# A hybrid backbone: where two groups of modulation weights and the latents are loaded in the opening stage

## The chip, the cores and the metric

The kernel runs on one core of one Trainium2 chip. The metric is the time of one execution on the device in microseconds, lower is better. The median of three runs of the kernel before is 4596.12 us (4592.82 to 4600.3). The profile is that of one further execution.

Five engines have instruction lists of their own and run them in order: TensorE (PE in the rows; PEld is its loading of weights), VectorE (DVE), ScalarE (ACT), GpSimd (POOL) and SyncE (SP). Transfers between memory and the core's own memory are issued either by SP (queue q1 in the rows) or by POOL (queue q0); the same 16 DMA engines move the bytes of both. An issue that has to wait, for a buffer for instance, holds back what stands behind it on its engine.

## The reference, cut to what matters

A two-layer backbone over 512 latent tokens x, with 256 context tokens in front, model width 1024, all in float32. Layer 0 mixes with a short convolution beside a state-space scan, layer 1 with a gated linear recurrence; an expert stage follows in each layer.

```
cond_x = silu(c); cond_c = silu(c_ctx)
mx = split(cond_x @ ada_w[layer] + ada_b[layer], 6)     # ada_w[layer]: 1024 x 6144
mc = split(cond_c @ ada_w[layer] + ada_b[layer], 6)
hx = modulate(rmsnorm(x,   norm_mix_w[layer]), mx[0], mx[1])
hc = modulate(rmsnorm(ctx, norm_mix_w[layer]), mc[0], mc[1])
ox, oc = even_mixer(hx, hc, ...)                         # layer 0
x   = x   + mx[2] * ox;   ctx = ctx + mc[2] * oc
x   = x   + mx[5] * peer_ffn(modulate(rmsnorm(x, ...), mx[3], mx[4]), ...)
ctx = ctx + mc[5] * peer_ffn(modulate(rmsnorm(ctx, ...), mc[3], mc[4]), ...)
```

Six vectors of 1024 are computed from each layer's modulation weights. The context's mixer needs the first two before anything else, the third when it adds its result, the last three only in the expert stage. The latents' mixer starts from the context's final states, so the context's mixer comes first.

## The kernel before, in words

**The opening.** The context (two tiles of 128 tokens, `cx`) is loaded, normed and transposed (`context_raw`, L274). The modulation weights of a layer are 24 MB and are handled in three groups of 2048 columns (`ada_group`, L242). Group 0 gives the first two vectors, group 1 the third and fourth, group 2 the fifth and sixth. A group has 16 tiles `adaw` of 128 x 1024 floats (0.52 MB each), with six buffers that all groups share, and two matmuls for each tile (L263), 32 in all; each has only the 32 columns of `cond` as its weights and writes one quarter of the rows of a PSUM tile. Then VectorE adds the bias (L265), and four small stores put the vectors into memory (`mods`). `context_mod` (L284) applies group 0 to the transposed context and splits it into a high and a low part (`hTch`, `hTcl`).

**The context's mixer** (`even_mixer`, L435, with 256 tokens). Every projection is three matmuls for a k (high by high, low by high, high by low; L229) with weights `ev_w_in` that are loaded into `wr` (four buffers) and split into `wh` and `wl` by ScalarE and VectorE (L199, L200). `even_steps` comes first (`step_sizes`, L361). Then, for each half: two groups of the state-space scan (`ssd`, L495: projections, transposes L515, L522, the decay terms L553 to L574, a group norm L589), the short convolution of four blocks (`short_conv`, L476: projections only), and the output projection (`out_proj`, L456, matmuls L469 with `ev_w_out`), whose gate needs group 1.

**What sets the order.** The program is traced in the order of the code, and a scheduler then puts each engine's instructions into an order of its own, by what depends on what and by its own idea of time. Two helpers bind it. `tc.issue_after(ins)` puts each instruction of its block behind `ins`, but only those on the same engine as `ins`. `between(todo, hooks)` (L305) spreads a list of pieces of work over calls of `hook` (L297); each `hook` follows an instruction of VectorE (in `ssd` L570, one for each of two tiles; in `short_conv` L493) and runs the pieces that are due in an `issue_after` of that instruction. `HA` (L29) is the number of hooks over which the pieces are spread.

In the kernel before, groups 1 and 2 are such pieces, with their tiles on SP's queue behind the last tile of group 0 (`rows` is that DMA); the latents' four tiles `x` are loaded by SP behind it as well. The latents are first read when their own mixer begins, after the context's.

Of the kernel before, what the change touches and what calls it, by code (L numbers as in the profile page):

```python
# [25 lines left out]
HF = 2  # L26
FD, TU = 0, 0
HB = 4
HA = 6  # L29
GA = (1, 3, 7)  # L30
NA0 = 12
NA1, NS1, W1, NR1, HS1, HS0, NE1 = 30, 8, 34, 6, 100, 96, 4
# [33 lines left out]
class Backbone:  # L66
# [1349 lines left out]
    def build(self):  # L1416
        tc, nc, io = self.tc, self.nc, self.io
        with ExitStack() as es:
# [7 lines left out]
            x = [hold.tile([128, D], F32, name=f"x{i}") for i in range(4)]  # L1426
            self.ctxd = [tc.dram_tile((T_C, D), F32, name=f"ctx{l}") for l in range(2)]

            @contextmanager
            def phase(bufs, raws=2):  # L1430

                with tc.tile_pool(name="wpool", bufs=bufs) as self.wpool:
                    self.rawp = self.wpool, raws
                    yield
# [51 lines left out]
            with phase(4, 4):  # L1486
                ada_pool = right("ada")
                C = ada_pool.__enter__()
                for i in range(2):
                    self.load(cx[i], io["ctx"][i * 128:(i + 1) * 128])  # L1490
                with tc.tile_pool(name="evenhc", bufs=1) as H:
                    with tc.tile_pool(name="prec0", bufs=1) as Q:
                        hT = self.split_pair(H, [128, KT, T_C], "hTc")
                        xT = self.context_raw(cx, Q)
                        ada = self.ada_group(0, 0, C, 6)
                        with tc.issue_after(ada.ins):
                            self.even_consts(H, T_C)
                            self.context_mod(xT, hT, Q)
                    rows = ada

                    def ada_group(l, j):
                        with tc.issue_after(rows.ins):
                            self.ada_group(l, j, C, 6)

                    self.between([lambda l=l, j=j: ada_group(l, j)
                                  for l, j in ((0, 1), (0, 2))], HA)
                    with Pools(tc, "evenc") as P:
                        with tc.issue_after(ada.ins):
                            steps = self.even_steps(hT, T_C, P, "c")
                        with tc.issue_after(rows.ins):  # L1510
                            for i in range(4):
                                self.load(x[i], io["x"][i * 128:(i + 1) * 128])
                        with tc.issue_after(ada.ins):
                            fin = self.even_mixer(hT, T_C, T_C, steps, None, cx, P, "c")
                self.dump("cm0", cx)
                for i in range(2):
                    self.load(self.ctxd[0][i * 128:(i + 1) * 128], cx[i])
                ada_pool.__exit__(None, None, None)
                ch = right("c_h")
                ctoks, hW = self.context_norm(E, ch.__enter__(), cx)  # L1520
# [83 lines left out]
```

## Time and profile before

| | |
|---|---|
| median of three runs | 4596.12 us |
| the profiled execution | 4590.89 us |
| its span, first to last instruction | 4589.1 us |
| TensorE busy | 4199.3 us, 92% of the span |
| VectorE, ScalarE, POOL busy | 3420.0, 1755.9, 1456.6 us |
| mean DMA rate | 244 GB/s |
| modulation tiles of layer 0, by SP | 48 of 0.52 MB |
| modulation tiles of layer 1, by POOL | 48 of 0.52 MB |

The change concerns the opening and the context's mixer, the first 330 us or so. In the rows, a matmul of 32-bit floats appears as two records (`x4` are two matmuls of L263), one of L229 as a single one. The shares of the whole span say little of this stage, so the rows below are of stretches of it.

### The profile page before, as it was taken

Reading aid. Unit: us, or ns where it says so; the run is one execution under the profiler, and the core shown is the slowest. Engines: PE = TensorE matmul, PEld = TensorE weight load, DVE = VectorE, ACT = ScalarE, POOL = GpSimd, SP = SyncE. Lnnn points to the kernel's source line nnn. Section 1 sums busy time; section 2 is a strip of 40 time slices with the busy share of each in tenths; the row PEclk is TensorE's granted clock in tenths of the full one; section 3 lists DMA queues with packets and bytes.
Section 4 is the critical chain, followed back from the end, with each engine's and each line's share of the span. In section 5 each row is a group of like instructions: output and inputs, shape, how many; then the busy total and the mean of one; then the engine's idle time right before and its main releaser. Section 6 shows DMA issues by size and latency. Waiting matters only on the chain. (4 is left out here: it accounts for less than half of the span.)

```text
span 4589.1 us, 60329 instructions
## 1 busy us (share of the span) xinstructions
PE 4199.3 (92%) x21452; PEld 3358.1 (73%) x21452; DVE 3420.0 (75%) x6826; ACT 1755.9 (38%) x3155; POOL 1456.6 (32%) x1114
## 2 busy tenths in 40 slices
PE   7999868868897889999999999998999999999998
PEld 5666635535443778888899988887757779888997
DVE  4556887786676989977888875666896558878887
ACT  4442321321223833333333345554447533333333
POOL 0002244444435355544545410000000005445543
PEclk9999979969998989999999999998999999999999
DMA  9538778878777899988988941111246758989886
GB/s 315 175 111 274 237 230 270 262 227 289 248 250 261 267 326 351 363 330 317 321 325 321 338 138 52 57 60 49 83 139 193 235 193 320 328 305 330 327 315 224
DMA packets 488766, 1119.52 MB, mean 244 GB/s; under 512 B 39792, under 2 KB 252336, under 8 KB 488464
## 3 DMA queue, kind: packets, MB, share of 16 engines
q1 hardware_dynamic: 334096, 553.55, 36.0%
q0 software_dynamic: 154368, 562.11, 34.9%
q8 instruction: 169, 2.77, 0.2%
q14 instruction: 133, 1.09, 0.1%
HBM read 1054.18 MB, written 60.82 MB: 243 GB/s over the span
## 5 line engine op out<-in xcount | busy, mean ns | idle before, releaser
L952 POOL DMA_INDIRECT g<-in_peer_u_dram,idx x256 | 372.4, 1455 | 923.1 <-DVE pre L1057 693.6
L229 PE MATMUL yp<-hTh,wh 128*128 128x384 f32 x1808 | 610.3, 338 | 12.9 <-ACT wh L199 11.7
L200 DVE TENSOR_TENSOR wl<-wr,wh 128x1024 fp32r<-128x1024 f32 x404 | 493.1, 1221 | 167.1 <-ACT wh L199 162.6
L229 PE MATMUL yp<-hTh,wl 128*128 128x384 f32 x1808 | 611.5, 338 | 5.4 <-DVE wl L200 5.2
L229 PE MATMUL yp<-hTl,wh 128*128 128x384 f32 x1808 | 608.1, 336 | 0.0
L199 ACT ACTIVATE wh<-wr 128x1024 fp32r<-128x1024 f32 x404 | 426.1, 1056 | 443.5 <-DMA wr<-in_peer_uT_dram 181.2
L952 POOL DMA_INDIRECT g<-in_peer_v_dram,idx x256 | 392.3, 1533 | 376.4 <-DVE y L1077 309.8
L952 POOL DMA_INDIRECT g<-in_peer_v_dram,idxc x256 | 339.1, 1325 | 392.4 <-DVE y L1077 172.9
L1057 DVE CUSTOM_DVE_ANT_0 g<-g,cx 128x1024 f32<-128x1024 f32 x256 | 312.7, 1223 | 148.3 <-DMA g<-in_peer_u_dram,idxc 145.9
L952 POOL DMA_INDIRECT g<-in_peer_u_dram,idxc x256 | 289.8, 1132 | 390.8 <-DVE prec L1057 343.5
L200 DVE TENSOR_TENSOR vl<-wr,vh 128x1024 fp32r<-128x1024 f32 x256 | 312.4, 1220 | 70.2 <-ACT vh L199 70.0
L229 PEld LDWEIGHTS yp<-hTh,wh 128*128 128x128 f32 x1808 | 341.5, 189 | 25.6 <-ACT wh L199 13.5
L229 PE MATMUL mm<-hTh,wh 128*128 128x512 f32 (+1 forms) x864 | 343.9, 399 | 17.3 <-ACT yT L579 8.6
L229 PEld LDWEIGHTS yp<-hTh,wl 128*128 128x128 f32 x1808 | 340.9, 189 | 13.1 <-DVE wl L200 10.1
L1057 DVE CUSTOM_DVE_ANT_0 g<-g,h 128x1024 f32<-128x1024 f32 x256 | 305.9, 1221 | 59.2 <-DMA g<-in_peer_u_dram,idx 59.0
L229 PEld LDWEIGHTS yp<-hTl,wh 128*128 128x128 f32 x1808 | 341.3, 189 | 8.9
L229 PE MATMUL mm<-hTh,wl 128*128 128x512 f32 (+1 forms) x864 | 342.1, 398 | 2.5 <-DVE wl L200 2.3
L229 PE MATMUL mm<-hTl,wh 128*128 128x512 f32 (+1 forms) x864 | 340.8, 395 | 0.2 <-DVE hTl L200 0.2
L1353 DVE TENSOR_TENSOR a<-a,gt 128x384 f32<-128x384 f32 x256 | 215.3, 845 | 167.3 <-ACT a L1241 91.4
L199 ACT ACTIVATE vh<-wr 128x1024 fp32r<-128x1024 f32 x256 | 270.2, 1055 | 173.4 <-PE mc L1375 76.4
L1077 DVE SCALAR_TENSOR_TENSOR y<-g,pre,y 128x1024 f32<-128x1024 f32 x254 | 325.1, 1280 | 13.0 <-DMA g<-in_peer_v_dram,idx 11.6
L88 POOL TENSOR_TENSOR rs_y<-rs_v,mhalf 128x1 f32<-128x1 f32 (+2 forms) x29 | 24.3, 839 | 929.6 <-DVE rs_v L87 929.5
(462 smaller groups left out, 9665.7 us busy)
## 6 DMA issues: line engine op xcount, KB each, us to landing
wr<-in_peer_v_dram SPq DMA_DIRECT2D x256, 512.0 KB
wr<-in_peer_uT_dram SPq DMA_DIRECT2D x226, 512.0 KB
gd<-stage SPq DMA_DIRECT2D x24, 2048.0 KB
gt<-gd SPq DMA_DIRECT2D x64, 768.0 KB
wr<-in_ev_w_in_dram SPq DMA_DIRECT2D x80, 512.0 KB
adaw<-in_ada_w_dram SPq DMA_DIRECT2D x48, 512.0 KB
adaw<-in_ada_w_dram POOLq DMA_DIRECT2D x48, 512.0 KB
wr<-in_peer_wq_dram SPq DMA_DIRECT2D x40, 512.0 KB
```

The costliest lines, as they stand in the source:

```text
L88: nc.gpsimd.tensor_tensor(y, v, self.mhalf[:, :n], op=OP.pow)
L199: self.nc.scalar.activation(hi, src, AF.Copy)
L200: self.nc.vector.tensor_sub(lo, src, hi.bitcast(F32))
L229: mm(o, a, rhs(kk, i)[b], start=first and kk == 0 and n == 0, stop=last and kk == k - 1 and n == 2)
L952: self.nc.gpsimd.indirect_dma_start(out=g, out_offset=None, in_=table, in_offset=bass.IndirectOffsetOnAxis(ap=idx, axis=0), element_offset ...
L1057: self.nc.vector.tensor_tensor_reduce(g, g, t.h2, 1.0, 0.0, OP.mult, OP.add, s["pre"][:, k, h:h + 1])
L1077: nc.vector.scalar_tensor_tensor(t.y, g, a, t.y, op0=OP.mult, op1=OP.add)
L1353: self.last = nc.vector.tensor_mul(a, a, self.gt_[:, :, i % 4])
```

## The change

```
-HA = 6
+HA = 12
...
-                    rows = ada
-
-                    def ada_group(l, j):
-                        with tc.issue_after(rows.ins):
-                            self.ada_group(l, j, C, 6)
-
-                    self.between([lambda l=l, j=j: ada_group(l, j)
-                                  for l, j in ((0, 1), (0, 2))], HA)
+
+                    def load_x():
+                        for i in range(4):
+                            nc.gpsimd.dma_start(x[i], io["x"][i * 128:(i + 1) * 128])
+
+                    self.between([lambda j=j: self.ada_group(0, j, C, 6, nc.gpsimd) for j in (1, 2)] + [load_x], HA)
                     with Pools(tc, "evenc") as P:
                         with tc.issue_after(ada.ins):
                             steps = self.even_steps(hT, T_C, P, "c")
-                        with tc.issue_after(rows.ins):
-                            for i in range(4):
-                                self.load(x[i], io["x"][i * 128:(i + 1) * 128])
```

The tiles of groups 1 and 2 are issued by POOL instead of SP, and the extra `issue_after` around them is gone. Three pieces (group 1, group 2, the latents) are spread over twelve hooks instead of two over six, so they are traced at hooks 1, 5 and 9. The latents' four loads are issued by POOL and are the third piece.

At the start of POOL's list, rows of the difference (`x_88` to `x_91` are the latents' tiles, `rs_y` belongs to the context's first norm):

```order
 L163 IOTA jp 128x128
 L182 IOTA iota_82 128x128
+L1502 DMA x_88<-in_x_dram 128x1024
+L1502 DMA x_89<-in_x_dram 128x1024
+L1502 DMA x_90<-in_x_dram 128x1024
+L1502 DMA x_91<-in_x_dram 128x1024
 L88 TENSOR_TENSOR rs_y<-rs_v,mhalf 128x2
 L341 IOTA iot 128x4
 L347 IOTA iop 128x1
+L262 DMA adaw<-in_ada_w_dram 128x1024 x32
```

The latents' loads are now the first transfers on POOL, and all tiles of groups 1 and 2 follow in one run.

On TensorE between the two groups of the scan in the first half (from the first group's norm L589 to the second group's L553), the kernel before:

```order
L589 MATMUL mc<-yT,ones 128x256 x2
L515 MATMUL mc<-ident,ch 128x128 x3
L263 MATMUL mm<-adaw,cond 32x512 x4
L522 MATMUL mc<-xe,tk 128x512
L515 MATMUL mc<-ident,ch 128x128 x3
L263 MATMUL mm<-adaw,cond 32x512 x4
L522 MATMUL mc<-xe,tk 128x512
L553 MATMUL mc<-ch 128x128
```

and the changed one:

```order
L589 MATMUL mc<-yT,ones 128x256 x2
L515 MATMUL mc<-ident,ch 128x128 x3
L522 MATMUL mc<-xe,tk 128x512
L515 MATMUL mc<-ident,ch 128x128 x3
L522 MATMUL mc<-xe,tk 128x512
L553 MATMUL mc<-ch 128x128
```

The matmuls of group 2 that stood between the scan's steps are gone from there. On TensorE at the start of the short convolution, and within it, the kernel before has projections only (the first rows; `mm_1344` is a PSUM tile):

```order
L589 MATMUL mc_1224<-yT_432,ones_80 128x256 x2
L229 MATMUL mm_1344<-hTch_127,wh_1304 128x256
L229 MATMUL mm_1344<-hTcl_128,wh_1304 128x256
L229 MATMUL mm_1344<-hTch_127,wl_1305 128x256
L229 MATMUL mm_1344<-hTch_127,wh_1304 128x256
```

and the changed one, a stretch in its middle (`mm_1329` is the PSUM tile of group 2):

```order
L263 MATMUL mm_1329<-adaw_1366,cond_99 32x512 x2
L229 MATMUL mm_1447<-hTch_127,wh_1442 128x256
L229 MATMUL mm_1447<-hTcl_128,wh_1442 128x256
L229 MATMUL mm_1447<-hTch_127,wl_1443 128x256
L229 MATMUL mm_1447<-hTch_127,wh_1442 128x256
L229 MATMUL mm_1447<-hTcl_128,wh_1442 128x256
L263 MATMUL mm_1329<-adaw_1370,cond_99 32x512 x2
```

Group 2 now stands among the projections of the short convolution: a run of twelve matmuls and then ten pairs. Before the first L561 the kernel before has 48 matmuls of groups 1 and 2 in 16 places (runs of 8, 6 and 4 among them) and 336 projection matmuls; the changed one has the 32 of group 1 there, as a run of twelve, eight pairs and a run of four, and 352 projection matmuls. On TensorE the sixteen transposes of the context (L128), which the kernel before mixes into group 0, now stand ahead of all of it.

## Rows read from the trace of the kernel before

**Rows 1.** Busy times by stretch: us, busy PE, PEld, DVE, ACT, POOL, PEclk, DMA share, GB/s

```profile
0.00:34.00 34.00, 19.87 (x80) 5.12 (x80) 5.64 (x27) 10.94 (x14) 1.54 (x9) 0.95 0.87 292
41.40:116.60 75.20, 70.54 (x471) 52.38 (x471) 36.29 (x69) 35.90 (x53) 0.00 (x0) 0.94 0.98 325
116.60:155.20 38.60, 31.89 (x222) 18.02 (x220) 20.87 (x40) 18.27 (x30) 0.00 (x0) 0.96 0.53 183
155.20:185.00 29.80, 29.76 (x248) 29.76 (x249) 20.19 (x33) 15.62 (x20) 0.00 (x0) 1.00 0.56 155
```

**Rows 2.** TensorE in order of time: start, us, then the wait before it

```profile
33.24 1.05 PE L263 MATMUL mm<-adaw,cond 128*32 128x512 f32 x4 [0.28 <-DMA adaw<-in_ada_w_dram]
...
39.41 0.39 PE L229 MATMUL mc<-hTch,wh 128*128 128x256 f32 x1 [2.79 <-ACT hTch L199]
...
116.68 0.38 PE L561 MATMUL mc<-trow,srow 15*128 15x512 bf16 x1
...
155.24 0.38 PE L229 MATMUL mm<-hTch,wh 128*128 128x256 f32 x1 [0.93 <-ACT scx L482]
...
185.09 1.45 PE L469 MATMUL mc<-wo,yT 128*128 128x512 f32 x3
```

**Rows 3.** Busy times of two short stretches

```profile
41.90:46.40 4.50, 4.50 (x23) 4.50 (x23) 3.60 (x8) 2.12 (x2) 0.00 (x0) 0.50 1.14 339
346.00:350.00 4.00, 4.00 (x14) 3.30 (x13) 3.75 (x7) 1.20 (x2) 3.54 (x7) 0.50 0.82 275
```

**Rows 4.** TensorE's waits from 41.5 to 185: us in total, times, longest

```profile
PE mc L589 <- ACT yT L586: 4.0, 2, 2.2
...
PE mm L229 <- ACT wh L199: 0.5, 1, 0.5
```

**Rows 5.** SP's and POOL's lists in order of time

```profile
7.49 0.71 POOL L88 TENSOR_TENSOR rs_y<-rs_v,mhalf 128x2 f32<-128x2 f32 x1 [6.21 <-DVE rs_v L87]
...
33.69 2.00 SPq L81 DMA_DIRECT2D x<-in_x_dram  x4
...
40.05 2.77 SPq L262 DMA_DIRECT2D adaw<-in_ada_w_dram  x3
...
346.29 3.44 POOL L262 DMA_DIRECT2D adaw<-in_ada_w_dram  x6 [0.18 <-issue]
```

**Rows 6.** ScalarE in order of time, the first use of the latents

```profile
339.46 1.04 ACT L111 ACTIVATE hin<-x 128x1024 f32<-128x1024 f32 x1
```

**Rows 7.** Busy times of two stretches of the opening

```profile
3.00:18.00 15.00, 8.14 (x32) 3.34 (x36) 3.62 (x14) 7.80 (x12) 0.92 (x3) 1.00 1.02 347
18.00:25.00 7.00, 3.90 (x24) 0.64 (x20) 0.00 (x0) 1.86 (x2) 0.00 (x0) 1.00 0.86 267
```

**Rows 8.** DMA queues from 350 to 356: packets, MB, share of 16 engines

```profile
q0 software_dynamic: 399, 1.47, 78.9%
q1 hardware_dynamic: 315, 0.41, 23.3%
```

**Rows 9.** TensorE in order of time, four and two modulation matmuls together

```profile
63.53 1.06 PE L263 MATMUL mm<-adaw,cond 128*32 128x512 f32 x8
...
74.05 1.05 PE L263 MATMUL mm<-adaw,cond 128*32 128x512 f32 x4
```

**Rows 10.** Busy times of L263 alone by stretch: PE, PEld, PEclk, DMA share, GB/s

```profile
41.40:116.60 75.20, 18.46 (x96) 2.87 (x96) 0.94 0.98 325
116.60:155.20 38.60, 6.06 (x34) 0.80 (x32) 0.96 0.53 183
```

**Rows 11.** TensorE and VectorE within the scan, in order of time

```profile
131.79 1.83 PE L589 MATMUL mc<-yT,ones 128*128 128x256 f32 x4 [2.16 <-ACT yT L586]
...
140.09 1.10 PE L522 MATMUL mc<-xe,tk 128*128 128x512 f32 x2 [1.83 <-DVE xe L520]
...
146.88 0.69 DVE L568 TENSOR_TENSOR E<-E,ch 128x512 f32<-128x512 f32 x1
...
149.94 0.66 PE L574 MATMUL yp<-E,tk 128*64 128x128 f32 x8
```

## The prediction

> **What bounds the kernel now.** I read the busy times by stage first [rows 1]. Up to 34 us TensorE works only 19.9 us of 34, while DMA moves 292 GB/s: the kernel waits for the first group of modulation weights. From 41.4 us to 185 us it is the other way round: TensorE is busy 70.5 of 75.2 us, then 31.9 of 38.6, then 29.76 of 29.8. In the first of these stretches DMA is nearly full as well (share 0.98, 325 GB/s), and still TensorE idles only 4.7 us in it. So the full DMA queues cost almost nothing there; TensorE's own list is the limit.
>
> Then I read TensorE's rows in order of time [rows 2]. The last matmuls of group 0 start at 33.24, held by their DMA; VectorE, a transpose and the modulation follow, and the first projection matmul starts at 39.41. Everything behind hangs on these times. From 41.9 to 46.4 the granted clock is 0.50 (1.2 GHz), after TensorE had mostly waited, and 23 matmuls take 4.5 us [rows 3], 0.20 each; from 155.2 to 185 it is 1.00 (2.4 GHz) and 248 take 29.76, 0.12 each [rows 1].
>
> The list of waits for 41.5 to 185 has seven lines, from 4.0 us down to 0.5 (the first and the last are [rows 4]); all but one name ScalarE or VectorE as releaser, one none, and no DMA stands in it. So there is no wait on TensorE's list that a relieved DMA queue would plainly remove.
>
> **The change, part by part.** From the first matmul with ev_w_out (L469) on, the order on TensorE is the same in both kernels for a long way, so I work out when that point comes; it is at 185.09 now.
>
> *The latents.* They are not loaded later. The four transfers wait for nothing, and the diff ties them to VectorE's hook only, not to POOL; they stand on POOL's queue behind two IOTAs, ahead of its first rs_y. A group of six such issues on POOL took 3.44 us [rows 5], so all four are issued by about 4 us. That rs_y starts at 7.49 today, so it is not delayed by the issues. In the kernel before, SP issues the latents at 33.69, behind group 0 [rows 5]. They are first read at 339.46 [rows 6], so neither place is late; but the new place puts 2.1 MB into the one stretch in which TensorE waits for DMA. At the 347 GB/s of the stretch from 3 to 18 us [rows 7] that is 6.0 us. Part is absorbed: at 18 to 25 us only 267 GB/s move, because buffers came free late behind transposes that the old order mixes into group 0; the new order puts all sixteen transposes first. 80 GB/s times 7 us is 0.56 MB, 1.6 us. Left: some 4 us.
>
> *Group 1 overtakes the tail of group 0.* Its tiles have the same six buffers, and POOL issues a tile as soon as TensorE has read the buffer. SP did that only at 40.05 [rows 5], since its list had other things first. Now the first tile of group 1 goes out when the eleventh of sixteen tiles of group 0 has been used, and the two queues share the DMA engines for the last five. The trace has such a stretch, 350 to 356: both queues had work, and moved 399 and 315 packets [rows 8], so about equal numbers; POOL's carried more bytes because its packets are bigger. With rows of 4 KB in both, equal packets are equal bytes, and some three of POOL's tiles of 0.52 MB get through early: 4.5 us at 347 GB/s. Since tiles are issued one by one I take half, 2 us. Bounds: nothing; all six tiles, 9 us. They are fetched for later, but nothing later needed them sooner.
>
> The Trainium skill ("DMA: Bandwidth & Descriptors", section "Queues, rings and completion order") states that each DMA engine goes round between the queues with work, a packet at a time. The packet counts of [rows 8] agree; by the byte shares there (78% to POOL) the sum would rise by some 4 us instead of 2.
>
> So the start moves by 4 + 2 = 6 us (bounds 1 and 13). VectorE and ScalarE split the first big weight inside the modulation now; I count that within these bounds.
>
> *Matmuls of groups 1 and 2.* Each group has 32, two per tile. Their 32 columns let up to four run together: four take 1.06 us (eight records at 63.53), two take 1.05 (four records at 74.05) [rows 9]. I count units, each of up to four matmuls in a row. Before the first L561, the old order has 18 units: 18.46 us [rows 10], 1.03 each. The new one has 12 there (a run of twelve counts three): -6.2 us. It has 352 instead of 336 projection matmuls there: +1.9 us. Of the 4.7 us of idle time in that stretch I take 1.5 away, since the new order puts more projection work ahead of its waits (bounds 0 and 4.7): -5.8 in all.
>
> *The state-space chain, 116.7 to 155.2.* The old order has 5 units and 48 projection matmuls in it (the units 6.06 us [rows 10]), the new one 32 projection matmuls and no unit. Most units stood where TensorE had to wait: it is held 2.16 us up to the L589 at 131.79 by ScalarE, and 1.83 up to the L522 at 140.09 by VectorE [rows 11], with a unit shortly before each. They were free, and go without gain. Others cost: 23 projection matmuls ran from 147.0 to the L574 at 149.94, whose second operand was ready at 147.57 (146.88 + 0.69 [rows 11]). I give the stretch -3 us (bounds 0 and -6).
>
> *The short convolution.* From 155.24 to 185.09 there are 248 projection matmuls and nothing else, with no gap. The new order has the same 248 and all of group 2 among them: a run of twelve and ten pairs, 3 + 10 = 13 units at 1.0: +13 us (12 to 15, if a tile or a weight is late). This is the cost that the change adds: group 2 leaves the gaps of the chain and goes into a stretch without gaps.
>
> *POOL's queue.* An adaw issue there waits for TensorE, and what stands behind it waits too: the next on POOL is the rs_y of the context's second norm, and group 2 must be done before that in any case. 32 issues of some 0.57 us (3.44 by six [rows 5]) are beside TensorE's work: 0.
>
> *The rest.* Small swaps of the order follow in the latents' mixer and the expert stage; I see no side in them: 0, plus or minus 4.
>
> Sum: 6 - 5.8 - 3 + 13 = **+10.2 us**. The profiled execution took 4590.89 us (span 4589.1 and 1.8 around it), which gives 4601.1; the median of the runs is 4596.12, 5.2 above it, so I say **4606 us**, 0.22% slower. About 0.2%, 9.2 us, is what a measurement of this kernel can tell from no change.
>
> **Rivals.**
>
> *The start is free* (20%). The latents fill holes and the overtaking is small, so the start moves by 1: the sum is +5, no measurable change, 4601. For it: 18 to 25 us is below the full rate [rows 7]. Against it: 0 to 34 us moved 9.9 MB (34 us at 292 GB/s [rows 1]), and 12 MB at 347 GB/s alone take 34.6 us. It decides at the last group-0 matmul: 33 to 35 us.
>
> *SP's weights starve* (10%). When a run of twelve frees six buffers, POOL queues 3.1 MB at once; by the bytes of [rows 8] SP is left with 22%, while the projections read 0.52 MB per 24 matmuls, 2.9 us, or 180 GB/s. Behind each run TensorE would wait for weights, some 5 us twice: +20, 4616. Against it: raw weights are four tiles ahead.
>
> *Faster: the queues were the hidden pace* (10%). TensorE's idle time from 41.4 to 155.2 is 4.7 + 6.7 = 11.4 us [rows 1]. If late weights feed all of it, relief takes it away; with a start that moves by 1, two more units (23 became 25, +2), and a clock that doesn't drop at 41.9 (23 matmuls in 2.8 us instead of 4.5, -2), the sum is 1 - 11.4 + 2 - 2 = -10.4, 4586. It decides at the L589 and L522 waits: they must go. Against it: their releasers are ScalarE and VectorE, on data that came from TensorE.
>
> *POOL's issues slow beside VectorE* would be worse too; I leave it in the 10% of the starving. Six issues took 3.44 us, 0.57 each, while VectorE was busy 3.75 of 4 us [rows 3, 5], so the sum holds nothing for it. The Trainium skill ("SBUF — State Buffer", section "SBUF: two separate sides") states that VectorE's two-port modes lock GpSimd out of writing descriptors; a subsection of it has 620 ns alone and 3100 beside such an operation. As an estimate by that figure an issue would take 2.9 us where the pairs in the convolution come every 2.2, and ten pairs would add 7 us; these rows show none of it.
>
> **How the numbers follow.** The forecast has 60%, with its own range from +3 to +18 (4599 to 4614); of it 0.38 lies over +9.2 and 0.22 under. Starving adds 0.10 to slower, the free start 0.20 to the same, the hidden pace 0.10 to faster. Slower 0.48, same 0.42, faster 0.10. The low bounds add to 1 - 9 - 6 + 12 = -2, with up to -4 from the rest; the high ones to 13 - 4 + 0 + 15 = +24. Leaving out the outermost: 4592 to 4618.
>
> **What would show it.** Right: POOL issues x near 1.3 us; the last group-0 matmul is at 37 to 42 instead of 33.24; the first L561 comes at 115 to 118; the first L469 at 192 to 199, and short convolution's 248 projection matmuls span 42 to 45 us. Wrong: L469 earlier than 188, or a later stage that gives back or adds more than 4 us.

## The result, and the profile after

The changed kernel takes 4627.98 us (median of five runs, 4623.4 to 4636.0), the kernel before beside it 4596.12 (4585.18 to 4600.3, five runs): a ratio of 1.0072, 95% interval 1.0056 to 1.0087. That is 32 us slower; the forecast was 10 us slower, and 4627.98 lies outside the range (4592 to 4618). The profiled execution took 4630.82 us (span 4629.0), 39.9 more than the profiled one of before.

Busy times of the changed kernel by stretch, cut at the same events as [rows 1] (the columns are the same): the opening, first L229 to first L561, the scan, the short convolution.

```profile
0.00:40.00 40.00, 17.99 (x80) 5.60 (x80) 5.64 (x27) 10.83 (x14) 6.64 (x18) 0.96 0.93 323
50.09:117.48 67.39, 64.94 (x456) 51.96 (x457) 39.12 (x76) 37.98 (x60) 8.56 (x16) 0.94 0.88 282
117.48:153.82 36.34, 26.22 (x174) 15.65 (x173) 20.07 (x38) 18.82 (x32) 0.00 (x0) 0.86 0.20 57
153.82:200.77 46.95, 45.88 (x313) 33.91 (x314) 21.90 (x35) 15.46 (x20) 5.33 (x10) 0.97 0.68 223
```

The second stage is 9.9 us shorter than before (67.39 against 77.27 from 39.41 to 116.68), the scan 2.2 shorter, the short convolution 17.1 longer. TensorE's rows that answer to [rows 2]:

```profile
39.52 1.05 PE L263 MATMUL mm<-adaw,cond 128*32 128x512 f32 x4 [0.92 <-DMA adaw<-in_ada_w_dram]
47.79 1.08 PE L289 MATMUL mc<-ident,adam 128*128 128x128 f32 x4 [7.22 <-DVE adam L268]
50.09 0.58 PE L229 MATMUL mc<-hTch,wh 128*128 128x256 f32 x1 [1.22 <-ACT hTch L199]
...
117.48 0.38 PE L561 MATMUL mc<-trow,srow 15*128 15x512 bf16 x1
...
153.82 0.58 PE L229 MATMUL mm<-hTch,wh 128*128 128x256 f32 x1 [0.93 <-ACT scx L482]
...
200.77 1.88 PE L469 MATMUL mc<-wo,yT 128*128 128x512 f32 x4
```

The last matmuls of group 0 start 6 us later than in [rows 2], as foreseen. The next row was not: TensorE waits 7.22 us for VectorE's L268 (it scales group 0's vectors; L289 transposes them), and the first projection comes at 50.09, 10.7 us late. The first L469 is 15.7 us late.

**What L268 waited for.** ScalarE, VectorE and the queues' issues (SPq, POOLq) of the changed kernel:

```profile
34.95 0.33 SPq L81 DMA_DIRECT2D arow<-in_ssd_a_log_dram  x1
...
46.48 0.23 ACT L321 ACTIVATE arow<-arow 128x32 f32<-128x32 f32 x1 [23.84 <-DMA arow<-in_ssd_a_log_dram]
...
40.62 0.69 DVE L265 TENSOR_TENSOR adam<-mm,adam 128x512 f32<-128x512 f32 x1 [30.55 <-PE mm L263]
46.74 0.18 DVE L322 TENSOR_SCALAR arow<-arow 128x32 f32<-128x32 f32 x1 [5.43 <-ACT arow L321]
46.95 0.69 DVE L268 SCALAR_TENSOR_TENSOR adam<-adam,adan 64x512 f32<-64x512 f32 x1
...
33.79 0.58 POOL L262 DMA_DIRECT2D adaw<-in_ada_w_dram  x1 [25.64 <-DMA adaw<-in_ada_w_dram]
...
40.88 0.54 POOL L262 DMA_DIRECT2D adaw<-in_ada_w_dram  x1 [1.44 <-PE mm L263]
```

L322 (the scan's `arow`, 16 KB, in the kernel before first used at 55 us) stands ahead of L268 on VectorE in both kernels. `arow` landed 11.5 us after its issue here. In the kernel before, SP issued it at 29.32 and ScalarE had it at 34.07, at most 4.75 us later and before the last matmuls of group 0 were done, so L268 did not wait for it:

```profile
29.32 0.33 SPq L81 DMA_DIRECT2D arow<-in_ssd_a_log_dram  x1
...
34.07 0.23 ACT L321 ACTIVATE arow<-arow 128x32 f32<-128x32 f32 x1 [14.19 <-DMA arow<-in_ssd_a_log_dram]
...
34.95 0.17 DVE L322 TENSOR_SCALAR arow<-arow 128x32 f32<-128x32 f32 x1
35.15 0.69 DVE L268 SCALAR_TENSOR_TENSOR adam<-adam,adan 64x512 f32<-64x512 f32 x1
```

The changed kernel's queues from 33 to 46 us (packets, MB, share) show what lay beside it: group 1's first six tiles.

```profile
q0 software_dynamic: 797, 2.94, 61.7%
q1 hardware_dynamic: 2260, 1.90, 43.5%
```

POOL's 797 packets are of 3.7 KB on average. Of the 3057 packets of both queues 1922 are under 512 bytes, nearly all of them SP's. From 38 to 44 us, when both queues had work all the time, they moved about equal numbers of packets and very unequal bytes:

```profile
q0 software_dynamic: 615, 2.24, 95.4%
q1 hardware_dynamic: 666, 0.06, 8.4%
```

So a constant of few bytes, cut into many packets, is many turns beside POOL's tiles.

**The latents do the same at the start.** `cond` is 8 KB, issued by SP at 1.64 in both kernels. ScalarE's first use of it, in the changed kernel and then before:

```profile
14.50 1.28 ACT L239 ACT_TABLE_LOAD   x1 [7.57 <-DMA cond<-in_cond_dram]
```

```profile
7.22 1.28 ACT L239 ACT_TABLE_LOAD   x1
```

Behind it on ScalarE stands L280, so the context's first transpose is at 17.11 instead of 11.72. The changed kernel's queues from 6 to 10 us show SP's bytes nearly at a stop, those of group 0 behind `cond` included:

```profile
q0 software_dynamic: 372, 1.35, 87.2%
q1 hardware_dynamic: 585, 0.00, 8.0%
```

**Later stages.** I took VectorE's instructions of the same line and tiles, the n-th of one kernel against the n-th of the other, and the median difference of their starts around a point. It is +14 from 360 to 600 us, 12.9 at 1650, 20.3 at 1740, 20.1 at 1960, 26.4 at 2100, 28.7 at 3600 and 39.4 at 4500 (within 20 us of each point). So in this pair of profiles more than half of the loss arises where I expected nothing. In dense down (L1375, the first expert stage) the scheduler has put TensorE's matmuls in another order, by the trace from 1980 to 2290 us; from there on, but for a few rows, the order is that of before, also at 3600 to 3800, where some 11 us more appear.

### The profile page after: what moved, and what is told of

It reads as the page before. It is cut to its first block, busy times and chain, and to the rows that moved or that the text cites. A ratio compares the mean times of both kernels' runs of the same rounds, so it can differ in the third digit from the quotient of the medians.

```text
span 4629.0 us, 60361 instructions
## 1 busy us (share of the span) xinstructions
PE 4214.3 (91%) x21452; PEld 3367.0 (73%) x21452; DVE 3422.7 (74%) x6826; ACT 1756.5 (38%) x3156; POOL 1479.9 (32%) x1150
## 5 line engine op out<-in xcount | busy, mean ns | idle before, releaser
L229 PE MATMUL yp<-hTh,wl 128*128 128x384 f32 x1808 | 612.6, 339 | 12.3 <-DVE wl L200 12.3
L229 PE MATMUL yp<-hTh,wh 128*128 128x384 f32 x1808 | 611.2, 338 | 8.1 <-ACT wh L199 6.9
L229 PE MATMUL yp<-hTl,wh 128*128 128x384 f32 x1808 | 608.8, 337 | 0.0
L229 PEld LDWEIGHTS yp<-hTh,wh 128*128 128x128 f32 x1808 | 342.3, 189 | 22.8 <-ACT wh L199 8.7
L229 PE MATMUL mm<-hTh,wh 128*128 128x512 f32 (+1 forms) x864 | 344.5, 400 | 14.1 <-ACT yT L579 9.0
L229 PEld LDWEIGHTS yp<-hTh,wl 128*128 128x128 f32 x1808 | 342.0, 189 | 19.5 <-DVE wl L200 16.7
L229 PEld LDWEIGHTS yp<-hTl,wh 128*128 128x128 f32 x1808 | 341.8, 189 | 8.9
L229 PE MATMUL mm<-hTh,wl 128*128 128x512 f32 (+1 forms) x864 | 341.0, 397 | 4.2 <-DVE wl L200 4.2
L229 PE MATMUL mm<-hTl,wh 128*128 128x512 f32 (+1 forms) x864 | 343.9, 398 | 0.2 <-DVE hTl L200 0.2
L1375 PE MATMUL mm<-vh,ah 128*128 128x512 f32 x768 | 303.0, 395 | 25.8 <-ACT vh L199 19.0
```

The source lines that it names most:

```text
L229: mm(o, a, rhs(kk, i)[b], start=first and kk == 0 and n == 0, stop=last and kk == k - 1 and n == 2)
L1375: ins = nc.tensor.matmul(acc[t][hlf], x[:, ts], y[:, hlf * 512:(hlf + 1) * 512], start=(i == 0 and n == 0), stop=(i == 127 and n == 2))
```

## The experiments

All times are medians; a ratio is against the kernel before on the same chip, with its 95% interval. It is worked out from all runs and can differ from that of the two medians by 0.1%. In this table, in us: start of the last group-0 matmul, gap from there to L289, first L229, length of the scan (first L561 to the short convolution), length of the short convolution, first L469, and the step, the growth of VectorE's shift between 1960 and 2100 us. The first two lines are means of four profiles each; the ratio of the second is that of e1's runs.

| kernel | ratio | last g0 | gap | L229 | scan | conv | L469 | step |
|---|---|---|---|---|---|---|---|---|
| before (with e5, e13, e15) | 1 | 33.3 | 2.3 | 39.1 | 38.1 | 31.2 | 185.8 | 0.6 |
| changed (with e1, e14, e16) | 1.0074 (1.0060, 1.0088) | 39.7 | 7.8 | 49.8 | 39.3 | 46.4 | 203.1 | 5.9 |
| e2 latents by SP | 1.0052 (1.0035, 1.0070) | 32.7 | 7.8 | 43.0 | 41.0 | 45.9 | 199.5 | 0.2 |
| e3 place alone | 1.0036 (1.0023, 1.0049) | 31.6 | 2.3 | 37.3 | 37.8 | 45.9 | 192.3 | 0.0 |
| e4 queue alone | 1.0008 (0.9995, 1.0021) | 32.2 | 7.8 | 42.3 | 48.2 | 31.3 | 188.2 | 0.7 |
| e6 latents alone | 1.0039 (1.0025, 1.0052) | 37.7 | 2.3 | 45.3 | 43.9 | 29.9 | 192.1 | 0.1 |
| e7 latents late | 1.0042 (1.0029, 1.0056) | 33.3 | 2.8 | 43.6 | 44.2 | 46.6 | 203.2 | -0.2 |
| e8 constants early | 1.0048 (1.0031, 1.0065) | 40.0 | 2.2 | 52.3 | 42.1 | 46.6 | 210.8 | 0.9 |
| e9 before, wide tiles | 1.0023 (1.0012, 1.0034) | 32.6 | 5.1 | 40.0 | 37.8 | 29.9 | 176.9 | 5.5 |
| e10 changed, wide tiles | 1.0006 (0.9991, 1.0021) | 37.5 | 7.5 | 48.5 | 40.7 | 41.7 | 192.2 | 5.6 |
| e11 wide, HA = 5 | 0.9995 (0.9984, 1.0006) | 34.3 | 5.1 | 41.7 | 39.2 | 32.4 | 181.2 | 1.3 |
| e12 = e9 again | 1.0010 (0.9997, 1.0022) | 33.3 | 5.0 | 40.6 | 38.5 | 32.4 | 179.9 | 3.8 |

**e1, the changed kernel again.** No edit.

> The changed kernel once more, unaltered, as the yardstick of the others on the same chip. Against the profile of before, everything in the first profile of the changed kernel is shifted by +15.7 us at the first L469, by +14.0 from 360 to 600 us, by +5 more at 1660 to 1740 us (dense down, L1375), by +8 more at 1960 to 2050 us, and by +10.6 more at 3600 to 3800 us. Theory A (the first three are laid down by the new order of the instructions, the last, where the order is equal, is not): the first three shifts come back within 3 us each, the last comes back somewhere between -5 and +11; time 4623 to 4632. Theory B (all the later shifts are what any shift of the opening does to the dense down stage by chance): the two at 1660 and 1960 us scatter as the last does.

4626.82 us. The step at 1960 to 2100 came back (5.8); 1650 to 1740 gave 3.2 where the first profile has 7.4, and 3600 to 3800 gave 2.0 instead of 11. So of these three only the first came back, and 21 us stood at the opening instead of 14. Theory A holds in part.

**e2, e3, e4, e6: one part at a time.** e2 (`x` by SP behind group 0, the third piece empty):

```
-                    self.between([lambda j=j: self.ada_group(0, j, C, 6, nc.gpsimd) for j in (1, 2)] + [load_x], HA)
+                    self.between([lambda j=j: self.ada_group(0, j, C, 6, nc.gpsimd) for j in (1, 2)] + [lambda: None], HA)
...
+                        with tc.issue_after(ada.ins):
+                            for i in range(4):
+                                self.load(x[i], io["x"][i * 128:(i + 1) * 128])
```

e3 is e2 with groups 1 and 2 on SP (no queue given, in an `issue_after` of `ada`). e4 is e2 with two pieces and `HA = 6`. e6 is the kernel before with `nc.gpsimd.dma_start` for `x`, unbound.

> As the changed kernel, but the latents are loaded by SP behind the last tile of group 0, as before; groups 1 and 2 stay with POOL, at the same hooks. On TensorE the order from the latents' mixer's end on is then word for word that of before, dense down included. Theory A (the late part of the loss is the other order of the dense down stage, the opening gives the rest): no shift is added from 1600 to 2300 us (0 plus or minus 3); the last matmul of group 0 is near 35 instead of 39.98, since the latents no longer share the DMA engines with group 0; the constants of the mixer still come late beside POOL's tiles, so the transposes of L289 are near 42; first L469 at 195 to 199; time 4602 to 4614. Theory B (a shift of the opening costs the dense down stage 10 to 25 us by chance): 4615 to 4630.

> The place alone: groups 1 and 2 at the changed kernel's hooks (the first and the fifth of twelve), but by SP behind group 0, and the latents by SP, as before. TensorE has group 2 as 13 units in the short convolution, none in the scan; its order in dense down is that of before. If the place costs what the prediction says: start at 39.4 as before, -6 before the first L561, -3 in the scan, +13 to +17 in the short convolution, first L469 at 189 to 194, time +4 to +9 (4600 to 4606). If the place is what set all of the changed kernel's loss: +20 to +32.

> The queue alone: groups 1 and 2 by POOL, but at the hooks of before (first and fourth of six), latents by SP. TensorE has 25 units before the short convolution and none in it. If POOL's tiles delay the mixer's small constants (arow): the gap between the last matmul of group 0 and L289 grows from 2.3 to 7 or 8 us, start +5 to +7, of which the projections give back about 4, short convolution as before at 30 us; first L469 at 185 to 189, time 0 to +5 (4596 to 4601). If the small constants come late for another reason (the latents in front of them): the gap stays at 2.3 and the time is that of before or better.

> The latents alone: the kernel before, with only the four loads of the latents issued by POOL, unbound, at the start. If they cost what they cost the changed kernel: first transpose of the context near 17 us instead of 11.7, last matmul of group 0 at 39 to 41 instead of 33.7 (+6 to +7), the gap to L289 as before (2.3, since no tiles of POOL's follow), first L469 at 189 to 192, time +4 to +8 (4597 to 4601). If the earlier relief of the queues at 33.7 gives it back: first L469 at 183 to 187, time within 2 us of before.

The three single edits add: 0.36% for the place, 0.08% for the queue (not told from none), 0.39% for the latents: 0.83%, and the whole has 0.74%. The sum of whole times says nothing of where they arise: of e6's 17 us only 6.3 stand at the first L469, and its list on TensorE is another one between 535 and 1350 us, behind the context's mixer. e4 shows the gap of 7.8 without the latents, e6 the late group 0 without POOL's tiles. (e4's scan of 48.2 us holds more work, 11 units and 96 projection matmuls.) e4 in TensorE's rows:

```profile
31.71 1.05 PE L263 MATMUL mm<-adaw,cond 128*32 128x512 f32 x4 [0.74 <-DMA adaw<-in_ada_w_dram]
39.97 1.08 PE L289 MATMUL mc<-ident,adam 128*128 128x128 f32 x4 [7.21 <-DVE adam L268]
```

The last group-0 matmul is not late here or in e2, so group 1 did not overtake group 0's tail at all; it overtook the small constants behind it. e2's time, 4615.7, lies above the 4602 to 4614 of theory A and at the lower end of theory B's. Theory A's own sign failed as well: VectorE's shift grew by 9 us from 1600 to 2300 us, not by 0 plus or minus 3, although the order there is that of before (e5, e13 and e15 grow by 3 to 6 against the same first profile). e3's time (4607.3) is a little above its range, e6's (4608.2) 7 us above, and its last group-0 matmul came at 37.7, not at 39 to 41; e4's (4595.0) is just under its range, but within 2 us of the 4592.9 measured for before beside it.

**e5, the kernel before again.** No edit.

> The kernel before once more, unaltered, for a second profile. Every changed kernel so far lies 5 us on average further behind the first profile of before after 1660 to 1740 us, and 5 us more after 3600 to 3800 us, with the order of before or without it. If the first profile of before was quick there by chance, this one lies behind it by 3 to 7 us in each of the two places, and makes them up elsewhere. If the changes in the opening cause it, this one lies within 2 us of it in both.

4594.89 us: 3.8 us behind the first profile between 1650 and 1740, 3.4 between 3600 and 3800, in the range foreseen. e13 lies behind it there too, by 4.0 and 5.1, e15 by -0.4 and 0.7. So the first profile was among the quicker ones there, with the same list, and a part of the 39.9 us is chance.

**e7, latents truly late.**

```
+                    def group(j):
+                        self.rows = self.ada_group(0, j, C, 6, nc.gpsimd)
...
                     def load_x():
+                        with tc.issue_after(self.rows.ins):
...
-                    self.between([lambda j=j: self.ada_group(0, j, C, 6, nc.gpsimd) for j in (1, 2)] + [load_x], HA)
+                    self.between([lambda j=j: group(j) for j in (1, 2)] + [load_x], HA)
```

> The changed kernel, but its latents really come late: their loads on POOL are bound behind the last tile of group 2. Groups 1 and 2 stay with POOL at the changed kernel's hooks. If late latents are worth nothing in themselves: as the kernel with the latents on SP (last matmul of group 0 near 32.7, gap to L289 of 7.8 us, first L469 at 196 to 200, time 4608 to 4618). If they matter: first L469 at 190 to 195, time 4600 to 4607.

4610.63 us, in the range for late latents that are worth nothing in themselves. The 5 us between it and e2 (4615.7, on another chip) are within the intervals. Two marks were missed: L469 was at 203.2, above the 196 to 200 expected, since the scan took 44.2, and the gap was 2.8 instead of 7.8. `arow`, issued at 28.82, was there by 34.80 this time; what came late was the first projection weight:

```profile
34.80 0.23 ACT L321 ACTIVATE arow<-arow 128x32 f32<-128x32 f32 x1 [14.81 <-DMA arow<-in_ssd_a_log_dram]
42.22 1.06 ACT L199 ACTIVATE wh<-wr 128x1024 fp32r<-128x1024 f32 x1 [7.20 <-DMA wr<-in_ev_w_in_dram]
```

**e8, constants early.** `self.even_consts(H, T_C)` stands ahead of `ada_group(0, 0, ...)` instead of behind it.

> The changed kernel, but the mixer's small constants (arow among them) are loaded before group 0's tiles. If arow's late landing beside POOL's tiles holds VectorE's L268 and with it L289: the gap between the last matmul of group 0 and L289 goes from 7.8 to 2 to 3 us, the first L229 comes 5 us earlier than in the changed kernel (45 to 47), of which the projections keep half or more: time 2 to 5 us under the changed kernel, 4621 to 4625. If something else is late (the bias, the weights): the gap stays above 5 us, and the time stays at 4627.

4617.34 us, under the 4621 to 4625 foreseen. The gap went to 2.2 as foreseen, but the first L229 came later than ever, at 52.25 instead of 45 to 47:

```profile
42.17 0.63 PE L289 MATMUL mc<-ident,adam 128*128 128x128 f32 x4 [1.61 <-DVE adam L268]
52.25 0.58 PE L229 MATMUL mc<-hTch,wh 128*128 128x256 f32 x1 [9.45 <-ACT hTch L199]
```

ScalarE's row ahead of it names the next in line, the first projection weight:

```profile
47.60 1.06 ACT L199 ACTIVATE wh<-wr 128x1024 fp32r<-128x1024 f32 x1 [27.59 <-DMA wr<-in_ev_w_in_dram]
```

So `arow` was the first of SP's transfers to hurt, not the only one: here and in e7 it was the first weight behind it that came late while POOL's six tiles were out. The time is 10 us under that of e1 all the same, although its opening ends later (210.8). Its order of dense down is that of before; whether that makes up the 10 us isn't shown.

**e9 and e10, wide tiles.** One tile of 128 x 2048 per k, in half the buffers, so that four matmuls run together:

```
-                if q % 2 == 0:
-                    w = P.tile([128, 1024], F32, name="adaw", tag="adaw", bufs=bufs)
+                if q == 0:
+                    w = P.tile([128, 2048], F32, name="adaw", tag="adaw", bufs=bufs // 2)
```

> The kernel before with modulation tiles of 128 x 2048 in three buffers in place of 128 x 1024 in six, for both layers: each tile feeds four matmuls that run together. Groups 1 and 2 are 12 units among the first projections and 4 in the scan, where before had 18 and 5. Its opening is that of before, but its order on TensorE in dense down (1650 to 2100 us) is nearly that of the changed kernel. The price of a unit, 1 us, gives -6 before the first L561, first L469 at 177 to 182. Theory A (that order of dense down costs 6 to 9 us between 1960 and 2400 us against the second profile of before): the gain goes there, time 4588 to 4598. Theory B (the order is innocent): nothing is added there, time 4580 to 4588.

> The changed kernel with the same wide tiles: 9 units among the first projections instead of 12, none in the scan, 8 in the short convolution instead of 13. If the short convolution pays 1 us for each unit: 46.7 us become 39 to 42, first L469 at 190 to 199 (200.8 and 206.4 in the two profiles of the changed kernel). If it pays for the wait of each tile instead: 45 us or more. The scan has no unit and runs at a low clock, 36 to 44 us. Dense down has the changed kernel's order in most of it: theory A adds 6 to 9 us between 1960 and 2400 us, theory B none; time 4612 to 4622 by A, 4604 to 4613 by B.

e9: 4599.57 us, slower than before although its opening ends 9 us sooner, and 2 us over theory A's range. e10: 4595.72 us, well under its 4604 to 4622. The wide tiles are in layer 1 too, and no run separates what they do there: e10's opening is 11 us shorter than the changed kernel's, its ratio 0.7% lower. The short convolution with 8 units for 13 takes 41.7 us for 46.4. L263 alone in it, in the changed kernel and then in e10 (PE, PEld, clock, DMA share, GB/s):

```profile
153.82:200.77 46.95, 13.30 (x64) 2.12 (x64) 0.97 0.68 223
```

```profile
150.53:192.20 41.67, 8.11 (x64) 1.47 (x64) 0.94 0.71 241
```

The price is by the unit: 13 at 1.02 us, 8 at 1.01.

**e11 and e12, the order of dense down by itself.** e11 is e9 with `HA = 5`: the opening has the same units in the same stages, and TensorE's list in dense down is that of before word for word. e12 is e9 unaltered, on the same chip.

> The kernel before with wide modulation tiles, and HA = 5 in place of 6: on TensorE the opening is that of the wide kernel run as e9, but for the place of some L574 among the projections, and the order in dense down (rows 6000 to 8200 of TensorE) is word for word that of the kernel before, where e9 has nearly that of the changed kernel. Theory A (the changed kernel's order of dense down costs 5 us between 1960 and 2100 us): the shift against before grows by 0 to 1.5 us there (e9 and the three profiles with the changed kernel's order: 5.5 to 6.3), and the time is 4 to 6 us under e9: 4588 to 4595; with the opening's gain of 5 to 8 us it is the kernel that can beat before. Theory B (the step there belongs to the wide tiles or to chance): it grows by 4 to 6 us here too, time as e9.

> The wide kernel of e9 (HA = 6) once more, unaltered, beside e11 on one chip. By A its shift grows by 5 to 6 us between 1960 and 2100 us again, and its time is 4 to 6 us over that of e11; by B the step comes and goes, and the two times are equal within 2 us.

4596.82 against 4601.26 us; the step is 1.3 against 3.8 (e9: 5.5). The direction is that of theory A and the difference of 4.4 us the size foreseen, though the two intervals overlap, e11's time is over its 4588 to 4595 and e12's step under its 5 to 6. Over all profiles the step is 3.8 to 6.3 in the seven with the changed kernel's order or nearly that, and -0.2 to 1.4 in the ten others, the first profile of before (the reference) left out. Waits of TensorE there, with the changed kernel's order (first the changed kernel, 1980 to 2126 us, then e9, 1961 to 2107):

```profile
PE mm L1375 <- ACT vh L199: 5.8, 1, 5.8
PE yp L229 <- DVE wl L200: 4.4, 2, 3.4
```

```profile
PE mm L1375 <- ACT vh L199: 5.6, 1, 5.6
PE yp L229 <- DVE wl L200: 3.9, 2, 3.4
```

and with the order of before (before, 1960 to 2100, then e11, 1965 to 2107):

```profile
PE yp L229 <- ACT wh L199: 5.9, 1, 5.9
PE mm L1375 <- DVE al L200: 2.5, 1, 2.5
```

```profile
PE yp L229 <- ACT wh L199: 6.3, 1, 6.3
PE mm L1375 <- DVE al L200: 3.7, 1, 3.7
```

The pattern goes with the order: 3.4 us for `wl` in the one, 2.5 to 3.7 for `al` in the other. It does not give the loss. Busy times of these windows, before and then the changed kernel (us, PE, PEld, DVE, ACT, POOL, clock, DMA share, GB/s):

```profile
1960.00:2100.00 140.00, 133.04 (x651) 118.90 (x652) 114.43 (x162) 50.83 (x67) 65.89 (x46) 0.98 0.89 326
1980.00:2126.00 146.00, 137.87 (x666) 124.07 (x667) 117.78 (x168) 51.87 (x69) 71.31 (x49) 0.95 0.88 317
```

TensorE idles 7.0 us in the one and 8.1 in the other (e11 9.3, e9 7.0); the longer window holds 15 more of its matmuls. VectorE's list differs in the seven profiles already ahead of 1960, so the step compares instructions that have changed places, and it overstates what TensorE loses there. A fairer mark are matmuls that stand at the same row of TensorE's list in all kernels: from one at 1567 us (by the first profile of before) to one at 1971 TensorE's list is the same in all, and from there to one at 2313 lies the stretch with the other order. In that stretch the shift grows by 1.7 to 5.6 us in the seven (mean 3.1) and by -2.3 to 3.4 in the eleven others, the reference among them at 0 (mean 0.8). From 1567 to 1971 it grows by 4.1 to 11.0 (mean 9.0) and by -1.3 to 8.2 (mean 4.1); over both, by 12.9 in e9 and 13.5 in e12 against 6.9 in e11. So the seven are slower here in the mean, but the ranges overlap in both stretches, and more of the difference lies ahead of TensorE's own changed rows than in them. That the order costs a few microseconds is likely; how many, and by which wait, isn't shown. From 1650 to 2400 us before's own stage takes 750 to 754 us in its four profiles, the changed kernel's 755 to 766.

**e13 to e16, two more profiles of each.** No edits.

> A third profile of the kernel before, to tell what belongs to the kernels from what one execution differs from another. If the two changed stages (the opening, and dense down between 1960 and 2100 us) carry the loss: the mean shift of the changed kernel's four profiles against the mean of the four of before is 16 to 19 us at 360 us, grows by 4 to 6 between 1960 and 2100, and the rest (360 to 1960 and 2100 to the end) adds less than 4 us in each part. If the loss goes on after that: the rest adds 8 to 12 us.

> A third profile of the changed kernel, for the same means: last matmul of group 0 at 39 to 42, the gap to L289 7.8, the scan 36 to 41 us by the clock that is granted there, the short convolution 46 to 47, first L469 at 200 to 207; +4 to +6 between 1960 and 2100 us.

> A fourth profile of the kernel before, as the third: first L469 at 183 to 187, scan 38 to 39 us, 0 to 1.5 us between 1960 and 2100 us against the first.

> A fourth profile of the changed kernel, as the third: first L469 at 200 to 207, +4 to +6 between 1960 and 2100 us.

They took 4604.22 and 4592.12 us (before), 4610.01 and 4620.02 (changed). Mean shift of the changed kernel's four profiles against the four of before: 17.6 us at 360, 14.9 at 1960, 20.1 at 2100, 25.8 at 4500. So the opening carries 17.6 of 25.8, and VectorE's step is 5.2. The stretch from 360 to 1960 gives back 2.7, the one behind 2100 adds 5.7, a little more than the 4 foreseen; single profiles of one kernel differ by 13 us (before) and 21 us (changed) at the end, so I don't call that a stage's loss. On TensorE's common rows the same means are 12.1 at 1567, 17.6 at 1971 and 20.7 at 2313: 5.5 us of the opening's loss are given back before dense down, and 8.6 are added in it. e14's last group-0 matmul came at 37.4, before the 39 to 42 foreseen, and e15's scan took 37.7 us, just under its 38 to 39.

No kernel tried is shown to beat before; e4, e10, e11 and e12 are not told from it.

## Why the prediction was wrong

*Start, +6: measured +10.7.* The last group-0 matmul came 6.3 us late as said, but not by its terms. The latents alone make it 4.4 (e6), the size of their term; by the rows of the queues they do so through a small transfer (`cond`) that stood beside them and not by their bytes alone, though no run moves `cond` by itself. The overtaking of group 0's tail, +2, is nothing (e2, e4: 32.7 and 32.2); what is left lies within the changed kernel's own spread (37.4 to 41.8), so that the total came right is luck. The step that failed is the sentence that counted VectorE's and ScalarE's work behind group 0 within the bounds: POOL's tiles made `arow` late, and L268 stands behind it on VectorE, +5.5 in the gap. The rival of SP's starving weights had the mechanism, but I placed it behind the runs of twelve in the middle of the mixer, where one wait of 1.1 us stands, and not at the end of group 0, where six buffers come free as well.

*Before the first L561, -5.8: measured -9.8* (means of four). TensorE's idle time fell from 6.3 us (77.27 less 71.00) to 2.5 (67.39 less 64.94), by 3.8 where I took 1.5: while the start waits, weights may gather. Its work fell by 6.1 where the units and projections gave 4.3: L229 took 48.8 us for its 352 matmuls and 49.0 for the 336 of before, so the 1.9 for more of them did not come. So most of the start's extra loss came back, and the first L561, at 117.48, is within 115 to 118 as foreseen, by two misses that cancel.

*The scan, -3: measured +1.2 in the mean.* This is the term of the opening that failed. The units were called free: "They were free, and go without gain." They took no time of their own, but the granted clock went with them. The scan of the changed kernel from its L589 on, in two of its rows:

```profile
130.80 1.13 PE L589 MATMUL mc<-yT,ones 128*128 128x256 f32 x4 [2.15 <-ACT yT L586]
...
135.58 2.04 PE L522 MATMUL mc<-xe,tk 128*128 128x512 f32 x2 [3.32 <-DVE xe L520]
```

In the kernel before such a pair took 1.10 to 1.12 (the second of them in [rows 11], at 140.09). In both kernels the clock falls to its lower level (0.50, 1.2 GHz) behind the L589 that waits for ScalarE, at 132.1 and 133.1. Before, TensorE is busy all the next 3.4 us, four modulation matmuls among them, and the clock is back at 1.00 (2.4 GHz). In the changed kernel it stays down for 10.3 us in the first profile and 20.4 in the three others, and TensorE is idle for about 4 us of them (before, then the first and the second profile of the changed kernel):

```profile
132.10:135.50 3.40, 3.40 (x15) 1.53 (x13) 1.10 (x3) 2.59 (x4) 0.00 (x0) 0.50 1.06 347
133.10:143.40 10.30, 6.35 (x12) 2.65 (x12) 5.01 (x14) 3.47 (x8) 0.00 (x0) 0.50 0.00 0
135.80:156.20 20.40, 16.76 (x69) 8.70 (x69) 10.24 (x23) 6.62 (x14) 0.00 (x0) 0.50 0.00 1
```

What that costs shows in one list of instructions: the changed kernel's scan took 36.34 us in the first profile and 40.34 in each of the others, 4.0 us more for 10 us more at the lower level. Over all eighteen profiles, the scan has 0.1 to 7.8 us at the lower level in the eight with modulation matmuls between the first group's L589 and the next group's L561, and 10.5 to 31.3 in the ten without. e6 is among the latter: its units all stand ahead of those waits, and its scan took 43.9 us at 0.84. No run moves these units alone. e3 has 9 us less work on TensorE in the scan than before (5 units, 24 projections, at the full clock) and is shorter by 0.3 us.

*The short convolution, +13: measured +15.2* (17.1 in the first pair). In the first pair 13.3 are the units; the first matmuls run at the lower clock (0.58 instead of 0.38 for the first), one tile is late by 1.1 us, and each return to the projections costs 0.1. The mean is less since two of before's profiles (e13, e15) had the lower clock at its start as well, 32.5 us for 29.9. The term was right in kind, its bounds (12 to 15) a little narrow.

*POOL's queue, 0: right.* Single issues took 0.54 us, six in a row 3.19 us. The Trainium skill ("SBUF — State Buffer", section "SBUF: two separate sides") gives a transfer that GpSimd issues five times the time while VectorE works in one of its two-port modes; no row here shows that, with VectorE at work in the same stretch (its 21.9 us of 46.95 in the short convolution), though the rows do not tell in which mode.

*The rest, 0 plus or minus 4: the step that failed outright.* It was put at nothing without a row. By the means on TensorE's common rows 8.6 us are added from 1567 to 2313 us, 3.1 of them where TensorE's own order is another one; its waits there don't explain them, and the cause stays open. A comparison of the two lists would have shown where to look: they differ in many places from 1980 to 2290 us on TensorE and already ahead of that on VectorE, far from the change, though it would not have given the size. "I see no side in them" gave no bound from a row.

In sum the forecast's +10.2 was for the opening, which has +17.4 at the first L469. Of the 7.2 us between them the start and the first projections together are 0.7; the scan is 4.2 and the short convolution 2.2. Behind the opening 5.5 us are given back, 8.6 added in dense down and 5 behind it, of which only a part of the 8.6 goes with the other order. The profiles' times differ by 26.4 us in the mean, the timed medians by 32 to 34: two of the changed kernel's four profiled executions (4610.01, 4620.02) are quicker than any of the ten runs behind its two medians. Where the other 5 to 8 us are stays open.

## What to carry to other kernels

Before large loads are put on a second queue, look at which small transfers of the first queue are under way then, and who stands behind their readers on each engine: the loss is not the bytes but the first of them that is needed. Work that fills TensorE's waits may hold its clock, so moving it out of a chain can leave the chain as long as it was. With a scheduler, compare the whole order of both kernels and profile each kernel more than once: a change of the opening can cost several microseconds thousands of instructions later, and a single pair of profiles gave 39.9 us where the means of four gave 26.4. And measure such a shift on instructions that stand at the same place in both lists: read on VectorE's moved instructions, one stretch seemed to lose 5 us; on TensorE's common rows most of the loss lay elsewhere.

## What the hardware showed

An 8-KB transfer issued at 1.64 was ready by 7.22 us when SP's queue was alone, and at 14.5 beside four 0.5-MB transfers of POOL's (12.3 to 14.5 in the changed kernel's four profiles); a 16-KB one took 11.5 us beside POOL's tiles and at most 4.75 without them, though the DMA engines moved 372 GB/s meanwhile. I had weighed the two queues by bytes and by packets of 4 KB, not by how many packets a small transfer has. One list of instructions took 36.3 or 40.3 us in the scan by the clock granted in it. And although both kernels have one order on every engine from 3300 us on, their first profiles drew 11 us further apart between 3600 and 3800, and with the second of the changed kernel it was 2.
